# A two-layer hybrid trunk on one core: half-height score passes grouped by head pair, gate rows at full height, and the query norm moved into Exp

## The chip, the cores and the metric

The kernel runs on one core of one Trainium2 chip. The metric is the device time of one execution in microseconds (us). Engines are named as in the profile: PE (TensorE matmul), PEld (its weight loads), DVE (VectorE), ACT (ScalarE), POOL (GpSimd), SP (the queue that issues most DMAs).

## The reference, cut to what matters

Two layers run over 256 latent tokens and 256 context tokens. In each layer three head groups stand side by side: a bidirectional mLSTM (4 heads), a neighbourhood attention with a position bias (NA, 6 heads), and a multi-head latent attention (MLA, 6 heads). Then come an output projection and a feed-forward block (dense in layer 0, top-2-of-8 experts in layer 1). Context outputs of the mixers are needed in layer 0 alone.

```python
# MLA: the queries' norm is one factor for each token
cq = rmsnorm(a[..., :Q_LORA], q_norm_w)          # y = x * rsqrt(mean(x*x) + EPS) * w
qf = (cq @ w_uq).reshape(b_, t_, MLA_H, MLA_NOPE + MLA_ROPE)
...
s_l = einsum(qn_b, kn) + einsum(qr_b, kr)        # latent keys
s_c = einsum(qn_b, knc) + einsum(qr_b, krc)      # context keys
pr = softmax(concatenate([s_l, s_c], -1))
# NA
s = einsum('bhqd,bhrkd->bhqrk', q_r, k_b) + bias
pr = softmax(concatenate([s, einsum('bhqd,bhcd->bhqc', q_r, kc)], -1))
# mLSTM
s = einsum('bhntd,bhnsd->bhnts', qc, kc) * exp(dmat - m_t[..., None])
```

## The kernel before, in words

Work is written in Python in one order, and a scheduler that knows the dependences lays out a fixed order for each engine. Each engine then runs its own list strictly from front to back. So where PE waits for data in a score pass, everything behind it on PE waits too; what keeps PE filled is projection work (the helper `mm3`, lines L93 to L95) which the scheduler puts between score passes and transposes.

Products are made of fp32r halves. For NA and the mLSTM a head has 64 dimensions. Its queries are kept as a tile of 128 rows (`hi`: 64 rows of high halves, 64 rows of low halves, made by `stack_q`), its keys as a tile of 128 rows (the high halves twice) and one of 64 rows (the low halves, made by `stack_k`). A score therefore takes two matmuls into the same PSUM bank: a **full-height pass** over 128 rows and a **half-height pass** over 64 rows. Head 0 of a pair has its half-height pass on rows 0 to 63, head 1 on rows 64 to 127. MLA scores are one fp32 matmul over 128 rows; the profile shows it as two records.

The attention of a pair of heads (`pair_attend`) runs, for each head and each half `tt` of the queries: score passes, softmax (`lat_probs`: maximum on DVE, Exp on ACT, reciprocal and scaling on DVE), four transposes on PE (`transp`, L377), and at the end the product with the values for both heads (`pv`, L364 and L370), in which head 0 writes PSUM rows 0 to 63 and head 1 rows 64 to 127. In layer 0 the context queries follow (`ctx_probs`). Score banks come from `bs`, a ring of two PSUM banks. Names of tiles tell group, layer, pair, head and half: `na0110s` is the score of NA, layer 0, pair 1, head 1, half 0; `na010cs` that of the context queries of head 0; `ma...` is MLA, `ml...` the mLSTM, `...t` a transpose.

The mLSTM needs, for each head and direction, one row of gate values on all 128 partitions: a matmul (`kbb`, L668) of a one-hot column with a 64-row tile `kbt`, 512 columns.

MLA's query norm is a column for each token (`rms_cols`: sums on PE, then eleven small DVE operations in `rstd`, L106 to L118). Before, `lora_rows` turned the column into a row on all partitions (four or two PE matmuls `cq..pr`, L340, and an ACT copy), and two tables `tab` were made of it on DVE (L819, L820). Every query tile is the projection times such a table (L830), so no MLA score can start before the norm is known.

Of the kernel before, what the change touches and what calls it, by code (L numbers as in the profile page):

```python
# [10 lines left out]
F32R = mybir.dt.float32r  # L11
# [3 lines left out]
OP = mybir.AluOpType  # L15
# [3 lines left out]
P = 128  # L19
# [53 lines left out]
def trunk(ctx: ExitStack, tc: tile.TileContext, I, out):  # L73
# [46 lines left out]
    class Stage:  # L120
# [264 lines left out]

        def lat_probs(self, q, k, tt, name, bias):
            s = self.bs(name + "s")
            for i in range(len(q)):
                pe.matmul(s, q[i][:, tt * P:(tt + 1) * P], k[i], start=(i == 0), stop=(i == len(q) - 1))
# [17 lines left out]
        def ctx_probs(self, q, k, name):  # L407
            s = self.bs(name + "s")
            for tt in range(2):
                for i in range(len(q)):  # L410
                    pe.matmul(s[:, tt * NL:(tt + 1) * NL], q[i][:, NL + tt * P:NL + (tt + 1) * P], k[i][:, NL:NT],
                              start=(i == 0), stop=(i == len(q) - 1))
            st = self.stat(name + "st")
            p = self.etile(name + "p")
            dve.tensor_reduce(st[:, 0:2], s.rearrange("p (t k) -> p t k", t=2), AX.X, OP.max, negate=True)
            for tt in range(2):
                c = slice(tt * NL, tt * NL + NL)
                act.activation(p[:, c], s[:, c], AF.Exp, bias=st[:, tt:tt + 1], accum_out=st[:, 4 + tt:5 + tt])
# [6 lines left out]
        def pair_attend(self, q, k, vt, vo, bias, full, name):  # L425
            pts, ptcs = [], []
            for i in range(2):
                pt = self.ptile(f"{name}{i}")
                for tt in range(2):
                    bb = None if bias is None else bias[i][:, (2 - 2 * tt) * 64:(6 - 2 * tt) * 64]  # L430
                    p = self.lat_probs(q[i], k[i], tt, f"{name}{i}{tt}", bb)
                    self.transp(pt, p, 4, tt, f"{name}{i}{tt}")
                pts.append(pt)
                if full:
                    ptc = self.ptctile(f"{name}{i}")
                    p = self.ctx_probs(q[i], k[i], f"{name}{i}c")
                    for tt in range(2):
                        self.transp(ptc, p[:, tt * NL:(tt + 1) * NL], 2, tt, f"{name}{i}c{tt}")
                    ptcs.append(ptc)
            o = self.bo(name + "o")  # L440
            n = self.pv(pts, ptcs, vt, vo, o)
            return o, n
# [45 lines left out]
        def layer(self, l, r, h=None, done=None):  # L488
# [167 lines left out]
            for j in range(2):  # L656
                pts, ptcs = [], []
                for i in range(2):
# [6 lines left out]
                    for d in range(2):  # L665
                        c = 4 * d + hd
                        kbb = self.bs(f"{nm}kb{d}")
                        pe.matmul(kbb, selr[:64, c:c + 1].to_broadcast([64, P]), kbt, start=True, stop=True)  # L668
                        dve.tensor_reduce(st[:, 4, d, 0:1], kbb[:, NL:NT], AX.X, OP.max)
# [8 lines left out]
                        if full:  # L678
# [7 lines left out]
                            ec.append(e)  # L686
                    for tt in range(2):
                        s = self.bs(f"{nm}s{tt}")
                        for u in range(2):
                            pe.matmul(s, q[u][:, tt * P:(tt + 1) * P], k[u], start=(u == 0), stop=(u == 1))  # L690
                        for d in range(2):
                            e = el[2 * d + tt]
                            dve.tensor_tensor_reduce(out=e, in0=s, in1=e, op0=OP.mult, op1=OP.add, scale=0.125, scalar=0.0,
                                                     accum_out=den[:, d, tt:tt + 1])
                    if full:
                        s = self.bs(f"{nm}sc")
                        for tt in range(2):
                            c = slice(tt * NL, tt * NL + NL)
                            for u in range(2):
                                pe.matmul(s[:, c], q[u][:, NL + tt * P:NL + (tt + 1) * P], k[u][:, NL:],  # L700
                                          start=(u == 0), stop=(u == 1))
                        for tt in range(2):
# [110 lines left out]
            ahead = [na_qk(j) for j in range(l)]  # L813
            rq = lora_rows(self.rms_cols(sq_, nq, 1.0 / 512, self.bs, f"cq{l}"), nq, self.bs, f"cq{l}")
            qs_ = 96.0 ** -0.5
            tabs = [self.ptmp(f"tab{l}{i}")[:, :nq] for i in range(2)]
            for i in range(2):
                a, b = slice(64 * i, 64 * i + 64), slice(64 - 64 * i, 128 - 64 * i)
                dve.tensor_scalar(tabs[i][a], rq[a], qs_, None, op0=OP.mult)  # L819
                dve.scalar_tensor_tensor(tabs[i][b], rq[b], qs_, ct[b, T_R:T_R + nq], op0=OP.mult, op1=OP.mult)  # L820
            for j in range(3):
# [3 lines left out]
                for i in range(2):  # L825
# [5 lines left out]
                    qs.append(t)  # L831
                o, n = self.pair_attend([[q] for q in qs], [[k] for k in K[2 * j:2 * j + 2]], vm, 128 * j, None, full, f"ma{l}{j}")
                mix[5 + j] = self.xbuf(f"ma{l}{j}x")[:, :n]
# [813 lines left out]
```

## Time and profile before

| what | value |
|---|---|
| median of 3 runs | 1792.4 us (1791.77 to 1795.92) |
| the profiled execution | 1796.54 us, span 1794.7 us |
| busy in the span | PE 1738.0 us (97%), PEld 1340.7, DVE 1358.0 (76%), ACT 1012.8 (56%) |
| mean granted PE clock | 0.990 |

Matmul ends are modelled, so PE busy includes cost that is not streaming; the start of one matmul to the start of the next is the better measure of what a matmul costs. The mixer of layer 0 runs from about 60 to 350 us, its feed-forward block to about 760 us, the mixer of layer 1 from about 773 to 1000 us, and the experts from there to the end.

### The profile page before, as it was taken

Reading aid. Unit: us, or ns where it says so; the run is one execution under the profiler, and the core shown is the slowest. Engines: PE = TensorE matmul, PEld = TensorE weight load, DVE = VectorE, ACT = ScalarE, POOL = GpSimd, SP = SyncE. Lnnn points to the kernel's source line nnn. Section 1 sums busy time; section 2 is a strip of 40 time slices with the busy share of each in tenths; the row PEclk is TensorE's granted clock in tenths of the full one; section 3 lists DMA queues with packets and bytes.
Section 4 is the critical chain, followed back from the end, with each engine's and each line's share of the span. In section 5 each row is a group of like instructions: output and inputs, shape, how many; then the busy total and the mean of one; then the engine's idle time right before and its main releaser. Section 6 shows DMA issues by size and latency. Waiting matters only on the chain.

```text
span 1794.7 us, 23711 instructions
## 1 busy us (share of the span) xinstructions
PE 1738.0 (97%) x8636; PEld 1340.7 (75%) x8636; DVE 1358.0 (76%) x2217; ACT 1012.8 (56%) x1418; POOL 3.0 (0%) x9
## 2 busy tenths in 40 slices
PE   6999999999999999999999999999999999999997
PEld 4776766778888888777767788768876787678886
DVE  4757756679987333477777699898989889998885
ACT  3545456542222222355656477786778677877774
POOL 0000000000000000000000000000000000000000
PEclk9999999999999999999999899999999999999998
DMA  9644202227787332322312769899999999999991
GB/s 299 230 156 129 83 25 70 72 72 236 224 314 239 94 94 83 125 91 74 95 56 67 283 257 353 349 420 388 343 372 410 390 350 348 416 410 352 341 361 70
DMA packets 82861, 410.08 MB, mean 228 GB/s; under 512 B 8912, under 2 KB 18640, under 8 KB 48944
## 3 DMA queue, kind: packets, MB, share of 16 engines
q1 hardware_dynamic: 82000, 406.62, 62.0%
q8 instruction: 70, 1.15, 0.3%
q0 software_dynamic: 304, 1.31, 0.2%
q10 hardware_dynamic: 432, 0.55, 0.1%
q14 instruction: 55, 0.45, 0.1%
HBM read 407.40 MB, written 1.05 MB: 228 GB/s over the span
## 4 chain that ended last, share of the span: by engine, by line
PE 85%; DVE 7%; ACT 4%; issue 2%; DMA 2%; SPq 0%; ACTq 0%; DVEq 0%; POOLq 0%
PE ah L1411 6%; PE ah L1412 6%; PE ah L1410 6%; PE ay L1470 3%; PE ay L1469 3%; PE ay L1471 3%; PE ah L1085 1%; PE ah L1088 1%; PE axgp L1265 1%; PE ah L1087 1%; PE ay L1088 1%; PE cq L93 1%; PE nk L93 1%; PE cq L95 1%; PE nk L95 1%
## 5 line engine op out<-in xcount | busy, mean ns | idle before, releaser
L262 DVE CUSTOM_DVE_ANT_0 junk<-awr,crow,sp 128x1024 f32<-128x1024 f32 x80 | 102.6, 1283 | 12.3 <-DMA awr<-adr 10.6
L1438 ACT CAST agh<-atr 128x256 fp32r<-128x256 f32 x55 | 20.5, 372 | 74.3 <-PE atr L1432 74.1
L1309 DVE SCALAR_TENSOR_TENSOR x<-asc,modT,x 128x256 f32<-128x256 f32 x64 | 27.3, 477 | 5.9 <-PE asc L1305 5.9
L1428 ACT ACTIVATE as<-ah 128x256 f32<-128x256 f32 x55 | 21.1, 383 | 10.3 <-PE ah L1412 9.7
L282 PE MATMUL ada<-aw,sc 128*32 128x128 f32 x256 | 13.5, 314 | 13.5 <-ACT Asq L299 11.9
L1324 ACT ACTIVATE ayy<-ay,gslot 128x512 fp32r<-128x512 f32 (+1 forms) x16 | 10.8, 674 | 25.7 <-PE ay L1471 17.5
L1336 ACT CAST aev<-ah 128x512 fp32r<-128x512 f32 x33 | 19.5, 592 | 9.8 <-PE ah L1085 8.0
L1075 DVE TENSOR_TENSOR am_13wl<-am_13w,am_13wh 128x2048 fp32r<-128x2048 f32 x8 | 18.3, 2292 | 7.3 <-ACT am_13wh L1074 7.3
L1075 DVE TENSOR_TENSOR am_21wl<-am_21w,am_21wh 128x2048 fp32r<-128x2048 f32 x8 | 18.3, 2292 | 7.2 <-ACT am_21wh L1074 7.2
L1271 ACT ACTIVATE axh<-axgp,modT 128x256 fp32r<-128x256 f32 (+1 forms) x40 | 16.1, 430 | 13.6 <-PE axgp L1265 10.0
L1439 DVE TENSOR_TENSOR agl<-atr,agh 128x256 fp32r<-128x256 f32 x55 | 23.0, 419 | 0.8 <-ACT agh L1438 0.8
L1429 DVE TENSOR_TENSOR as<-as,ah 128x256 f32<-128x256 f32 x55 | 22.8, 414 | 0.0
L1075 DVE TENSOR_TENSOR am_3wl<-am_3w,am_3wh 128x2048 fp32r<-128x2048 f32 x8 | 18.3, 2286 | 5.6 <-ACT am_3wh L1074 5.6
L282 PEld LDWEIGHTS ada<-aw,sc 128*32 128x32 f32 x256 | 7.3, 121 | 19.6 <-ACT Asq L299 11.9
L1075 DVE TENSOR_TENSOR av_28wl<-av_28w,av_28wh 128x2048 fp32r<-128x2048 f32 x8 | 18.3, 2289 | 4.2 <-ACT av_28wh L1074 4.2
L1075 DVE TENSOR_TENSOR am_11wl<-am_11w,am_11wh 128x2048 fp32r<-128x2048 f32 x8 | 18.3, 2288 | 4.0 <-ACT am_11wh L1074 4.0
L1075 DVE TENSOR_TENSOR av_30wl<-av_30w,av_30wh 128x2048 fp32r<-128x2048 f32 x8 | 18.3, 2286 | 3.5 <-ACT av_30wh L1074 3.5
L1432 PE MATMUL atr<-ck,as 128*128 128x128 f32 x110 | 20.9, 272 | 0.0
L1432 PEld LDWEIGHTS atr<-ck,as 128*128 128x128 f32 x110 | 15.3, 140 | 7.3 <-DVE as L1429 0.4
L1074 ACT CAST am_3wh<-am_3w 128x2048 fp32r<-128x2048 f32 x8 | 15.3, 1907 | 9.6 <-PE ah L1412 5.9
L1075 DVE TENSOR_TENSOR am_2wl<-am_2w,am_2wh 128x2048 fp32r<-128x2048 f32 x8 | 18.3, 2287 | 2.7 <-ACT am_2wh L1074 2.7
L1075 DVE TENSOR_TENSOR av_29wl<-av_29w,av_29wh 128x2048 fp32r<-128x2048 f32 x8 | 18.3, 2287 | 2.5 <-ACT av_29wh L1074 2.5
(6437 smaller groups left out, 6424.7 us busy)
## 6 DMA issues: line engine op xcount, KB each, us to landing
awr<-adr SPq DMA_DIRECT2D x56, 512.0 KB, 4.6
aw<-ada SPq DMA_DIRECT2D x24, 512.0 KB, 5.0
aw<-ada SPq DMA_DIRECT2D x32, 256.0 KB, 6.0
am_0w<-m SPq DMA_DIRECT2D x8, 1024.0 KB, 6.1
am_1w<-m SPq DMA_DIRECT2D x8, 1024.0 KB, 6.5
am_2w<-m SPq DMA_DIRECT2D x8, 1024.0 KB, 6.4
am_3w<-m SPq DMA_DIRECT2D x8, 1024.0 KB, 7.9
am_4w<-m SPq DMA_DIRECT2D x8, 1024.0 KB, 8.3
```

Source lines behind the costliest of these rows:

```text
L93: pe.matmul(ps, a[0], b[0], start=first, stop=False)
L95: pe.matmul(ps, a[1], b[0], start=False, stop=last)
L262: ins = dve.tensor_tensor_reduce(out=junk, in0=w, in1=rows[v], op0=OP.mult, op1=OP.add, scale=1.0, scalar=sp[:, l, b:b + 1], accum_out=mod ...
L1075: dve.tensor_tensor(l[:, c], raw[:, c], f32(h[:, c]), op=OP.subtract)
L1088: pe.matmul(p, x, w[1], start=False, stop=last)
L1410: pe.matmul(p, xh, wH, start=(kt == 0), stop=False)
L1411: pe.matmul(p, xh, wL, start=False, stop=False)
L1412: pe.matmul(p, xl, wH, start=False, stop=(kt == KT - 1))
L1432: pe.transpose(tr[:, u * P:(u + 1) * P], s[:, u * P:(u + 1) * P], ident)
L1469: pe.matmul(yq, gh, wH, start=(f == 0), stop=False)
L1470: pe.matmul(yq, gh, wL, start=False, stop=False)
L1471: pe.matmul(yq, gl, wH, start=False, stop=(f == NF - 1))
```

## The change

It has three parts.

1. **Score passes.** `lat_scores` and `ctx_scores` issue the passes of several scores together: first all full-height ones, then all half-height ones, tied in this order. For NA a group is both heads of a pair and one half of the queries; for the mLSTM it is both halves of one head; the context queries of NA form one group for both heads. A group takes both score banks.
2. **Gate rows.** `kbt` gets 128 rows (the rows added are zeros), and `kbb` is a full-height matmul of the same 512 columns.
3. **MLA's query norm.** `lora_rows` falls away for the queries, `tab` is made of constants alone, and the reciprocal rms `rq` of the query tokens is the `scale` of Exp. The negated maximum has to be multiplied by it first, one DVE operation on one or two columns for each softmax.

```diff
+        def lat_scores(self, items, name):
+            ss = [self.bs(f"{name}{i}") for i in range(len(items))]
+            n = len(items[0][0])
+            self.passes([(s, q[u][:, tt * P:(tt + 1) * P], k[u], u == 0, u == n - 1)
+                         for u in range(n) for s, (q, k, tt) in zip(ss, items)])
+            return ss
+        def ctx_scores(self, items, name):
...
+            self.passes([(s[:, tt * NL:(tt + 1) * NL], q[u][:, NL + tt * P:NL + (tt + 1) * P], k[u][:, NL:],
+                          u == 0 and tt == 0, u == n - 1 and tt == 1)
+                         for u in range(n) for tt in range(2) for s, (q, k) in zip(ss, items)])
...
-                dve.tensor_reduce(st[:, 0:1], s, AX.X, OP.max, negate=True)
-                act.activation(p, s, AF.Exp, bias=st[:, 0:1], accum_out=st[:, 4:5])
+                dve.tensor_reduce(st[:, 1:2], s, AX.X, OP.max, negate=True)
+                dve.tensor_tensor(st[:, 0:1], st[:, 1:2], rq, op=OP.mult)
+                act.activation(p, s, AF.Exp, bias=st[:, 0:1], scale=rq, accum_out=st[:, 4:5])
...
+            both = len(q[0]) > 1
+            for hds in ([(0, 1)] if both else [(0,), (1,)]):
+                for tt in range(2):
+                    ss = self.lat_scores([(q[i], k[i], tt) for i in hds], f"{name}{hds[0]}{tt}s")
+                    for i, s in zip(hds, ss):
+                        lat(i, tt, s)
...
-            kbt = self.tp.tile([64, 512], F32R, tag="kbt", bufs=1, name=f"kbt{l}")
-            act.mul(kbt, self.ct[:64, :512], 0.0)
+            kbt = self.tp.tile([P, 512], F32R, tag="kbt", bufs=1, name=f"kbt{l}")
+            act.mul(kbt, self.ct[:, :512], 0.0)
...
-                        pe.matmul(kbb, selr[:64, c:c + 1].to_broadcast([64, P]), kbt, start=True, stop=True)
+                        pe.matmul(kbb, selr[:, c:c + 1].to_broadcast([P, P]), kbt, start=True, stop=True)
...
-            rq = lora_rows(self.rms_cols(sq_, nq, 1.0 / 512, self.bs, f"cq{l}"), nq, self.bs, f"cq{l}")
+            rq = self.rms_cols(sq_, nq, 1.0 / 512, self.bs, f"cq{l}")
...
-                dve.tensor_scalar(tabs[i][a], rq[a], qs_, None, op0=OP.mult)
-                dve.scalar_tensor_tensor(tabs[i][b], rq[b], qs_, ct[b, T_R:T_R + nq], op0=OP.mult, op1=OP.mult)
+                dve.tensor_scalar(tabs[i][a], ct[a, T_R:T_R + nq], 0.0, qs_, op0=OP.mult, op1=OP.add)
+                dve.tensor_scalar(tabs[i][b], ct[b, T_R:T_R + nq], qs_, None, op0=OP.mult)
```

The mLSTM's own two score loops are replaced by `lat_scores` over its two halves and `ctx_scores` of one head.

Two places show how the engines' lists move. The first is PE in NA of layer 0, the context scores of pair 1. Before, `nk01h` (128 rows) and `nk01l` (64 rows) take turns:

```order
L411 MATMUL na010cs<-nk01h_2716,nq01h_2755 128x256
L411 MATMUL na010cs<-nk01l,nq01h_2755 128x256
L411 MATMUL na010cs<-nk01h_2716,nq01h_2755 128x256
L411 MATMUL na010cs<-nk01l,nq01h_2755 128x256
L389 MATMUL na0110s<-nk01h_2720,nq01h_2758 128x512
```

Of the change, the same scores (`_2856` is head 0, `_2857` head 1; the `nq` rows are projection work):

```order
L390 MATMUL na010cs_2856<-nk01h_2727,nq01h_2766 128x256
L93 MATMUL nq_2959<-h004h,nq02wh 128x512
L94 MATMUL nq_2959<-h004h,nq02wh 128x512
L95 MATMUL nq_2959<-h004h,nq02wl 128x512
L390 MATMUL na010cs_2857<-nk01h_2731,nq01h_2769 128x256
L390 MATMUL na010cs_2856<-nk01h_2727,nq01h_2766 128x256
L390 MATMUL na010cs_2857<-nk01h_2731,nq01h_2769 128x256
L390 MATMUL na010cs_2856<-nk01l,nq01h_2766 128x256
L390 MATMUL na010cs_2857<-nk01l,nq01h_2769 128x256
L390 MATMUL na010cs_2856<-nk01l,nq01h_2766 128x256
L390 MATMUL na010cs_2857<-nk01l,nq01h_2769 128x256
```

The four half-height passes of both heads now stand together, head 0 (rows 0 to 63) and head 1 (rows 64 to 127) in turn.

The second place is the start of MLA in layer 1 on DVE. Before (`cq1r` is the norm as a row, `q_7473` and `q_7488` the projections of the first pair's two heads):

```order
L118 SCALAR_TENSOR_TENSOR cq1rc<-cq1rc 128x2
L191 TENSOR_TENSOR nk11wl<-nk11w,nk11wh 128x1024
L819 TENSOR_SCALAR tab_7461<-cq1r 64x256
L820 SCALAR_TENSOR_TENSOR tab_7461<-cq1r,ctB 64x256
L819 TENSOR_SCALAR tab_7462<-cq1r 64x256
L820 SCALAR_TENSOR_TENSOR tab_7462<-cq1r,ctB 64x256
L830 TENSOR_TENSOR q100t<-q_7473,tab_7461 128x256
L830 TENSOR_TENSOR q100t<-q_7488,tab_7462 128x256
```

Of the change, from the first query tile on:

```order
L858 TENSOR_TENSOR q100t<-q_7479,tab_7467 128x256
L574 SCALAR_TENSOR_TENSOR nq10h_7449<-nq_7421,nq10h_7449 64x256
L112 SCALAR_TENSOR_TENSOR cq1rc<-cq1rc 128x2
L113 SCALAR_TENSOR_TENSOR cq1rc<-cq1rc 128x2
L114 TENSOR_TENSOR cq1rc<-cq1rc 128x2
L858 TENSOR_TENSOR q100t<-q_7494,tab_7468 128x256
L115 TENSOR_TENSOR cq1rc<-cq1rc 128x2
L116 TENSOR_SCALAR cq1rc<-cq1rc 128x2
L117 TENSOR_TENSOR cq1rc<-cq1rc 128x2
L415 TENSOR_REDUCE ma1000st<-ma1000s_7510 128x1
L118 SCALAR_TENSOR_TENSOR cq1rc<-cq1rc 128x2
L191 TENSOR_TENSOR nk11wl<-nk11w,nk11wh 128x1024
```

The query tiles no longer stand behind `cq1rc` (the eleven operations of the norm) and the tables, but among them. The new multiplication of the maximum (L416) is the next row, behind the weight split `nk11wl`.

On PE at this place `cq1pr` and twelve projection matmuls of the next pair (`q110`) stood ahead of `ma1000s`; now `ma1000s` and `ma1001s` follow the second head's projection directly, and those matmuls stand behind them. The DMA queue of SP moves four transfers by a few places and nothing else.

## Rows read from the trace of the kernel before

**Rows 1.** The page, section 4: shares of the chain that ended last, by engine.

```profile
PE 85%; DVE 7%; ACT 4%; issue 2%; DMA 2%; SPq 0%; ACTq 0%; DVEq 0%; POOLq 0%
```

**Rows 2.** Windows: stretch, length, busy PE PEld DVE ACT POOL, PE clock, DMA share, GB/s.

```profile
100.00:350.00 250.00, 248.68 (x1284) 172.10 (x1283) 171.83 (x522) 142.59 (x322) 0.00 (x0) 1.00 0.26 83
908.90:913.00 4.10, 4.03 (x9) 2.18 (x10) 1.92 (x5) 0.78 (x2) 0.00 (x0) 0.58 0.22 85
913.00:1000.00 87.00, 86.42 (x525) 62.10 (x524) 61.22 (x167) 54.99 (x139) 0.00 (x0) 1.00 0.26 82
```

**Rows 3.** Timeline of PE, NA of layer 0 (start, duration, ..., [idle before]).

```profile
277.84 0.39 PE L389 MATMUL na0000s<-nk00h,nq00h 128*128 128x512 f32 x1
278.16 0.49 PE L389 MATMUL na0000s<-nk00l,nq00h 64*128 64x512 f32 x1
278.58 0.50 PE L389 MATMUL na0001s<-nk00h,nq00h 128*128 128x512 f32 x1
279.01 0.50 PE L389 MATMUL na0001s<-nk00l,nq00h 64*128 64x512 f32 x1
279.44 0.50 PE L93 MATMUL nk<-h004h,nk01wh 128*128 128x512 f32 x1
279.79 0.40 PE L94 MATMUL nk<-h004h,nk01wh 128*128 128x512 f32 x1
280.02 0.39 PE L95 MATMUL nk<-h004h,nk01wl 128*128 128x512 f32 x1
```

**Rows 4.** Timeline of PE, two gate rows of layer 1 that follow each other.

```profile
812.06 0.28 PE L95 MATMUL mo<-h106h,mo11wl 128*128 128x256 f32 x1
812.27 0.73 PE L668 MATMUL ml10kb<-kbt,selr 64*128 64x512 f32 x2
812.92 0.50 PE L93 MATMUL kv<-h100h,kv10wh 128*128 128x512 f32 x1
813.27 0.39 PE L94 MATMUL kv<-h100h,kv10wh 128*128 128x512 f32 x1
```

**Rows 5.** Timeline of PE, products with the values, mLSTM, layer 0.

```profile
206.36 0.38 PE L364 MATMUL ml01o<-ml02pt,vml 128*64 128x256 f32 x1
206.37 0.38 PE L364 MATMUL ml01o<-ml03pt,vml 128*64 128x256 f32 x1
206.58 0.38 PE L364 MATMUL ml01o<-ml02pt,vml 128*64 128x256 f32 x1
```

**Rows 6.** Line 690, weight loads: count, ns min/median/max, first and last start.

```profile
L690 PEld LDWEIGHTS ml00s<-cv02sl,cv00sh x2: 183/183/183, 109.9 to 114.9; 64*128 64x128 f32 x2
```

**Rows 7.** Timeline, start of MLA in layer 1.

```profile
904.67 0.36 PE L93 MATMUL q<-cq10h,wq11wh 128*128 128x256 f32 x1
905.87 1.23 DVE L191 TENSOR_TENSOR nk11wl<-nk11w,nk11wh 128x1024 fp32r<-128x1024 f32 x1 [0.36 <-ACT nk11wh L190]
908.97 1.64 PE L389 MATMUL ma1000s<-K,q100t 128*128 128x512 f32 x2 [1.88 <-DVE q100t L830]
910.65 0.69 DVE L393 TENSOR_REDUCE ma1000st<-ma1000s 128x1 f32<-128x512 f32 x1 [1.17 <-PE ma1000s L389]
911.38 0.69 ACT L394 ACTIVATE ma1000p<-ma1000s,ma1000st 128x512 f32<-128x512 f32 x1 [4.69 <-DVE ma1000st L393]
912.97 0.15 DVE L403 RECIPROCAL ma1000st<-ma1000st 128x1 f32<-128x1 f32 x1
```

**Rows 8.** The chain in order of time (start, length, what), where Rows 7 end.

```profile
913.29 0.11 PE q L93
913.41 0.86 PE ma1010s L389 x2
```

**Rows 9.** Timeline, start of MLA in layer 0.

```profile
212.55 1.16 PE L340 MATMUL cq0pr<-ck,cq0rc 128*128 128x128 f32 x8
213.46 0.47 PE L93 MATMUL q<-cq01h,wq01wh 128*128 128x512 f32 x1
218.46 1.13 PE L389 MATMUL ma0000s<-K,q000t 128*128 128x512 f32 x2 [0.43 <-DVE q000t L830]
```

More of the change, by code (lines that the diff above doesn't have):

```diff
@@ L384, in ptctile, with passes, lat_probs @@
             return self.tp.tile([P, 2, NL], F32, tag="ptc", bufs=2, name=name + "ptc")
[L386 to L389, printed above, removed]
+        def passes(self, todo):
+            before = None
+            for out, lhs, rhs, first, last in todo:
+                ins = pe.matmul(out, lhs, rhs, start=first, stop=last)
+                if before:
+                    tc.add_manual_dep(ins.ins, before.ins.name, mybir.DependencyInfo(
+                        mybir.DependencyClass.NoSync, mybir.DependencyReason.DATA), reason="in order")
+                before = ins
+        def lat_scores(self, items, name):
[5 more added lines that the diff above has]
+        def ctx_scores(self, items, name):
+            ss = [self.bs(f"{name}{i}") for i in range(len(items))]
+            n = len(items[0][0])
+            self.passes([(s[:, tt * NL:(tt + 1) * NL], q[u][:, NL + tt * P:NL + (tt + 1) * P], k[u][:, NL:],
+                          u == 0 and tt == 0, u == n - 1 and tt == 1)
+                         for u in range(n) for tt in range(2) for s, (q, k) in zip(ss, items)])
+            return ss
+        def lat_probs(self, s, name, bias, rq=None):
             st = self.stat(name + "st")
@@ L405, in lat_probs, with ctx_probs @@
             return p
[L407 to L412, printed above, removed]
+        def ctx_probs(self, s, name, rq=None):
             st = self.stat(name + "st")
@@ L415, in ctx_probs @@
             dve.tensor_reduce(st[:, 0:2], s.rearrange("p (t k) -> p t k", t=2), AX.X, OP.max, negate=True)
+            if rq is not None:
+                dve.tensor_tensor(st[:, 2:4], st[:, 0:2], rq, op=OP.mult)
             for tt in range(2):
                 c = slice(tt * NL, tt * NL + NL)
-                act.activation(p[:, c], s[:, c], AF.Exp, bias=st[:, tt:tt + 1], accum_out=st[:, 4 + tt:5 + tt])
+                if rq is None:
+                    act.activation(p[:, c], s[:, c], AF.Exp, bias=st[:, tt:tt + 1], accum_out=st[:, 4 + tt:5 + tt])
+                else:
+                    act.activation(p[:, c], s[:, c], AF.Exp, bias=st[:, 2 + tt:3 + tt], scale=rq[:, tt:tt + 1],
+                                   accum_out=st[:, 4 + tt:5 + tt])
             dve.reciprocal(st[:, 8:10], st[:, 4:6])
@@ L423, in ctx_probs, with pair_attend, lat, ctx_ @@
             return p
[L425 to L428, printed above, removed]
-                for tt in range(2):
[L430 to L433, printed above, removed]
-                if full:
[L435 to L439, printed above, removed]
+        def pair_attend(self, q, k, vt, vo, bias, full, name, rq=None):
+            pts, ptcs = [self.ptile(f"{name}{i}") for i in range(2)], []
+            def lat(i, tt, s):
+                bb = None if bias is None else bias[i][:, (2 - 2 * tt) * 64:(6 - 2 * tt) * 64]
+                p = self.lat_probs(s, f"{name}{i}{tt}", bb, None if rq is None else rq[:, tt:tt + 1])
+                self.transp(pts[i], p, 4, tt, f"{name}{i}{tt}")
+            def ctx_(i, s):
+                p = self.ctx_probs(s, f"{name}{i}c", None if rq is None else rq[:, 2:4])
+                for tt in range(2):
+                    self.transp(ptcs[i], p[:, tt * NL:(tt + 1) * NL], 2, tt, f"{name}{i}c{tt}")
+            if full:
+                ptcs = [self.ptctile(f"{name}{i}") for i in range(2)]
+            both = len(q[0]) > 1
[4 more added lines that the diff above has]
+                        lat(i, tt, s)
+                if full:
+                    for i, s in zip(hds, self.ctx_scores([(q[i], k[i]) for i in hds], f"{name}{hds[0]}cs")):
+                        ctx_(i, s)
             o = self.bo(name + "o")
@@ L686, in layer @@
                             ec.append(e)
[L687 to L690, printed above, removed]
+                    ss = self.lat_scores([(q, k, tt) for tt in range(2)], f"{nm}s")
+                    for tt, s in enumerate(ss):
                         for d in range(2):
@@ L695, in layer @@
                     if full:
[L696 to L701, printed above, removed]
+                        s, = self.ctx_scores([(q, k)], f"{nm}sc")
                         for tt in range(2):
@@ L831, in layer @@
                     qs.append(t)
-                o, n = self.pair_attend([[q] for q in qs], [[k] for k in K[2 * j:2 * j + 2]], vm, 128 * j, None, full, f"ma{l}{j}")
+                o, n = self.pair_attend([[q] for q in qs], [[k] for k in K[2 * j:2 * j + 2]], vm, 128 * j, None, full, f"ma{l}{j}", rq)
                 mix[5 + j] = self.xbuf(f"ma{l}{j}x")[:, :n]
```

## The prediction, made before the change ran

> **What bounds the kernel now.** I read the chain of waits first. It runs through PE for 85% of the span [rows 1]. Then I read windows over the mixers, where the change lies: in layer 0, from 100 to 350 us, PE is busy 248.68 of 250 us at full clock, DVE 172, ACT 143; at the end of layer 1's mixer 86.42 of 87 us [rows 2]. The DMA engines are a quarter busy there. So what counts is what PE's list costs, and where it stands still. For that I read the timeline from start to start, since a busy PE may be one that streams nothing.
>
> Full-height passes of 512 columns that follow each other start 0.23 us apart (279.79 to 280.02) [rows 3]. Where a half-height pass stands between them the steps are 0.32, 0.42, 0.43, 0.43 and 0.35: from 277.84 to 279.79 five passes take 1.95 us in place of 5 x 0.234 = 1.17. No row of these has idle time in brackets. Two excursions to half height cost 0.78, so one costs 0.39 and one change of shape 0.195. That it is the change and not the half-height pass itself which costs is seen in the gate rows: from 812.06 to 813.27 stand one pass of 256 columns and three of 512, 0.82 us of streaming, and the time is 1.21: again 0.39 more, though two half-height passes lie in this one excursion [rows 4].
>
> **The change, part by part.** I counted shapes over PE's whole list. Stretches of half-height passes fall from 74 to 33: the gate rows lose theirs, NA has one for each group in place of one for each pass, and so has the mLSTM. The products with the values and other narrow ones are split up five times more. All changes of shape together fall from 293 to 227. The 66 fewer, at 0.195 each: **-12.9 us**. The bounds: 0.165, if the step of 0.35 after the return is left out (1.60 - 4 x 0.234 = 0.66 for four changes), and 0.20, the excess of a step of 0.43 [rows 3]: -10.9 to -13.2.
>
> Passes of two heads on opposite halves of the rows have no row in this trace. The nearest are the products with the values, in which two heads use opposite halves of the columns: the second starts 0.01 us behind the first, and the next couple 0.21 later [rows 5]. So I let such half-height passes share their time: in PE's list eight couples of 512 columns stand side by side (four more are parted by transposes), and six of 256. 8 x 0.22 + 6 x 0.11 = **-2.4 us**; the other end is 0. The Trainium skill ("TensorE: Matmul & The Clock Gate", Part 3 on packing small matmuls) gives about 4 ns between starts on different row groups; no run here shows it yet.
>
> The gate rows at full height stream the same 512 columns, so the matmul itself costs what it did. Clearing 128 rows in place of 64 is one ACT operation for each layer, over the same columns: 0.
>
> MLA, layer 1: PE waits 1.88 us before `ma1000s` for the query tile, which on DVE stands behind the norm, a weight split of 1.23 us and the tables [rows 7]. Then the clock is down: 0.58 on average from 908.9 to 913 [rows 2], that is mostly the lower of the two levels (1.2 of 2.4 GHz), right behind the 1.88 us in which PE stood still. From 904.67, where the next pair's projection starts, to `ma1010s` at 913.41 go 8.7 us [rows 7, 8]. Of the change, two scores of 0.86 and 18 passes of 0.12 lie in between [rows 8]: 3.9 us. A new wait takes some back. The bank of `ma1010s` comes free when the Exp of `ma1000s` is done, and that stands behind the maximum (0.69), the split `nk11wl` (1.23) and the new multiplication (0.15, the price of the reciprocal), then takes 0.69 [rows 7]: from 905.7, some 3.2 us with the last of the norm and the gaps, to about 909.1, where PE is ready at 908.6. 0.5 us there, about 0.4 before the first transposes, and 0.1 of latency: 8.7 - 3.9 - 1.0 = **-3.8 us**. Bounds: 0 (the stall comes back at the bank) and -4.8.
>
> MLA, layer 0: the matmuls of `cq0pr` fall away (212.55 to 213.46), and the wait of 0.43 before `ma0000s` [rows 9]: -1.3. But the norm of the mLSTM's second pair now stands on DVE among the first softmaxes, eleven operations of 0.15, so I take **-1.0**; bounds +1 and -1.3.
>
> The new multiplication stands in 30 softmaxes (18 in layer 0, 12 in layer 1) between the maximum and Exp. At 0.15 [rows 7] that is 4.5 us if nothing covers it. What covers it are projection matmuls and the other scores on PE; it is bare where a bank is waited for. Between 0 and +4.5 I take a third: **+1.5**.
>
> Groups take both score banks, so the second full-height pass waits until the bank before last has been read, and PE's list waits with it: projections, transposes, and behind them the ACT copies and the products with the values. There are 27 groups (12 and 3 in NA, 8 and 4 in the mLSTM). The scheduler puts projection work between the two full-height passes, as the order of `na010cs` shows. The nearest price is the 0.43 that a score waits for DVE in [rows 9], and in [rows 3] no score waits at all. One group in eight with 0.43: **+1.5**. Bounds: 0 and 0.43 in half of them, +6.
>
> Sum: -12.9 - 2.4 - 3.8 - 1.0 + 1.5 + 1.5 = -17.1. The profiled execution took 1796.54 us, so its like would take 1779.4. The median of the runs is 4.1 us below the profiled execution; against it I forecast 1792.4 - 17.1 = **1775.3 us**. What is saved reaches the end: the feed-forward block and the experts follow the mixers and are no shorter or longer for starting sooner.
>
> **The rivals.**
>
> *Half-height passes do not share (1780).* If the second head's pass waits for the first, the 2.4 us are gone. If in addition a weight load cannot hide behind a pass on the same rows, each of the mLSTM's 12 groups, which have two half-height passes on the same rows, pays a load of 0.18 [rows 6]: +2.2. For this stands that no couple on row halves has run here. Against it stands that full-height passes start 0.23 apart though each has a load of its own, so loads do hide behind passes on the same rows [rows 3], and that the two gate rows on the same rows cost no more than one excursion [rows 4]. 1775.3 + 4.6 = 1779.9. The Trainium skill has such a rule (the same page and part: loads overlap matmuls in flight only when the row group differs); the rows contradict it as far as they go.
>
> *The price lies in the half-height pass, not in the change of shape (1784).* Then grouping saves nothing and the gate rows alone gain, 14 of the 74 stretches, 12 of them single: 14 x 0.39 = 5.5 in place of 12.9, and no time is shared: -5.5 - 3.8 - 1.0 + 3.0 = -7.3, so 1785. [Rows 4] speak against it, with one place.
>
> *The score banks become the limit (slower).* A bank is held for a maximum and an Exp, 0.69 each, some 1.4 us [rows 7]. Before, one score was computed while the other was read. If the scheduler's cover is misjudged and each of 27 groups waits a whole hold, that is 38 us in place of the 1.5: 1775.3 + 36 = 1812. It ends slower than before if a group waits on average over 17.1 + 1.5 = 18.6 / 27 = 0.7 us, half a hold. For it speaks that PE's order is fixed and that ACT and DVE often have other work first; against it the projection work in between, and that DVE and ACT have a third of the mixers' time free [rows 2].
>
> *The gain is given back later (1788).* The fixed orders downstream were laid out anew too. If a transfer or a weight split there is what ends a wait, most of the 17 us turns into a longer wait: a quarter left, 1788. Against it: DMA engines are a quarter busy in the mixers [rows 2], and DMA is 2% of the chain [rows 1].
>
> **How the numbers follow.** The forecast 0.63, with its own range from 1771 (the best ends: -13.2, -2.4, -4.8, -1.3, and no waits) to 1780; no sharing 0.13; price in the pass 0.08; banks 0.08, half of it at or above the time before; given back 0.08. The range reaches from 1767 (the best ends, less the 4 us by which runs of one kernel lie apart) to 1785: it holds the first three cases, about 0.82. Changes under 0.3% (5.4 us, 1787.0 to 1797.8) can't be told from none. Faster: the first three, and part of the others, 0.87. Same: most of the given back and some of the banks, 0.09. Slower: the rest of the banks, 0.04.
>
> **What the profile will show.** Right: couples of half-height scores of NA that start 0.01 us apart; steps of 0.23 through each group and 0.32 to 0.43 only at its edges; `cq..pr` gone; `ma1000s` of layer 1 without a bracket, and the clock at 1.00 behind it. The mixer of layer 0 would be about 10 us shorter, that of layer 1 about 7. Wrong: brackets before the second full-height pass of a group, with DVE or ACT named; half-height passes of the two heads 0.2 apart; a lower clock somewhere in the mixers, where PE has come to stand still.

## The result, and the profile after

| | median | range, runs | against the kernel before |
|---|---|---|---|
| before | 1793.77 us | 1791.77 to 1795.92, 4 | |
| changed | 1780.57 us | 1777.92 to 1782.26, 4 | 0.9924, 95% interval 0.9912 to 0.9936 |

The kernel is 13.2 us faster (1793.77 - 1780.57), 4 us less than the 17.1 of the sum; 1780.57 lies inside the range given. The profiled execution took 1782.26 us. The page of the profile after, first its busy times, then the chain by engine, which answers to [rows 1]:

```profile
PE 1722.5 (97%) x8624; PEld 1336.2 (75%) x8624; DVE 1359.9 (76%) x2247; ACT 1013.7 (57%) x1416; POOL 3.0 (0%) x9
PE 85%; DVE 6%; ACT 5%; DMA 2%; issue 1%; SPq 0%; ACTq 0%; DVEq 0%; POOLq 0%
```

PE is 15.5 us less busy (1738.0 before), DVE and ACT as busy as before, and PE holds the chain as it did. Windows after, which answer to [rows 2]:

```profile
100.00:350.00 250.00, 248.22 (x1318) 175.54 (x1315) 175.98 (x545) 146.89 (x324) 0.00 (x0) 1.00 0.27 87
...
894.50:897.90 3.40, 3.40 (x14) 2.88 (x13) 2.25 (x11) 1.42 (x2) 0.00 (x0) 0.50 0.28 111
898.00:901.30 3.30, 3.26 (x22) 2.43 (x20) 2.94 (x7) 0.87 (x2) 0.00 (x0) 1.00 0.07 10
901.30:988.00 86.70, 85.20 (x521) 61.68 (x522) 62.32 (x177) 55.75 (x139) 0.00 (x0) 1.00 0.27 86
```

In the same 250 us of layer 0 PE runs 34 records more (1318 for 1284). In layer 1 a stretch at the lower of the clock's two levels (0.50, 1.2 of 2.4 GHz) has moved: it runs from 894.5 to 897.9, ahead of `ma1000s` (896.72, below) and into that score; from 898.0 on the clock is at 1.00.

The timeline of PE after, an NA group of layer 0, which answers to [rows 3]:

```profile
275.31 0.40 PE L95 MATMUL nk<-h004h,nk01wl 128*128 128x512 f32 x1
275.54 0.39 PE L390 MATMUL na0000s<-nk00h,nq00h 128*128 128x512 f32 x1
275.86 0.49 PE L390 MATMUL na0000s<-nk00l,nq00h 64*128 64x512 f32 x2
276.29 0.50 PE L93 MATMUL nk<-h006h,nk01wh 128*128 128x512 f32 x1
276.62 0.39 PE L94 MATMUL nk<-h006h,nk01wh 128*128 128x512 f32 x1
```

The two half-height passes stand in one row (x2); listed one by one they start at 275.86 and 275.87, 0.01 us apart as forecast. From their start to the next pass go 0.43 us, which was the step of one such pass in [rows 3], and from 275.54 to 276.62 four passes take 1.08 us, 0.14 more than 4 x 0.234.

The timeline of PE after, gate rows of layer 1, which answers to [rows 4]:

```profile
804.79 0.28 PE L95 MATMUL mo<-h106h,mo11wl 128*128 128x256 f32 x1
804.90 0.62 PE L702 MATMUL ml10kb<-kbt,selr 128*128 128x512 f32 x2
805.36 0.39 PE L93 MATMUL kv<-h100h,kv10wh 128*128 128x512 f32 x1
805.59 0.39 PE L94 MATMUL kv<-h100h,kv10wh 128*128 128x512 f32 x1
```

From 804.79 to 805.59 are 0.80 us for 0.82 of streaming; in [rows 4] it was 1.21.

The timeline after, start of MLA in layer 1 (PE, DVE and ACT), which answers to [rows 7, 8]:

```profile
891.42 1.23 DVE L191 TENSOR_TENSOR wq12wl<-wq12w,wq12wh 128x1024 fp32r<-128x1024 f32 x1
892.67 0.69 DVE L562 CAST nk10h<-nk 64x512 fp32r<-64x512 f32 x1
893.38 0.69 DVE L563 TENSOR_TENSOR nk10l<-nk,nk10h 64x512 fp32r<-64x512 f32 x1
894.22 0.36 PE L93 MATMUL q<-cq10h,wq10wh 128*128 128x256 f32 x1 [1.97 <-DVE nk10l L563]
896.72 1.60 PE L390 MATMUL ma1000s<-K,q100t 128*128 128x512 f32 x2
899.03 1.22 DVE L191 TENSOR_TENSOR nk11wl<-nk11w,nk11wh 128x1024 fp32r<-128x1024 f32 x1
900.16 0.15 DVE L416 TENSOR_TENSOR ma1000st<-ma1000st,cq1rc 128x1 f32<-128x1 f32 x1
900.35 0.78 ACT L417 ACTIVATE ma1000p<-ma1000s,ma1000st,cq1rc 128x512 f32<-128x512 f32 x1 [2.52 <-DVE ma1000st L416]
901.27 1.12 PE L390 MATMUL ma1010s<-K,q100t 128*128 128x512 f32 x2
```

`ma1000s` has no bracket any more. But an earlier wait is still there: a pass of the first pair's second projection waits 1.97 us for a bank that `stack_k`'s operations of `nk10` read on DVE, behind a weight split of 1.23. It stood in the trace before too, and the prediction passed over it:

```profile
903.18 0.35 PE L93 MATMUL q<-cq10h,wq10wh 128*128 128x256 f32 x1 [1.97 <-DVE nk10l L529]
913.25 0.59 PE L389 MATMUL ma1010s<-K,q100t 128*128 128x512 f32 x1
```

From there to `ma1010s` went 10.07 us; now it is 7.05 (901.27 - 894.22). The waits of PE after, in layer 1's mixer (us in total, times, longest):

```profile
PE q L93 <- DVE nk10l L563: 2.0, 1, 2.0
PE na1101t L377 <- DVE na1111st L425: 0.8, 1, 0.8
PE ml120t L377 <- DVE ml12e L745: 0.7, 1, 0.7
PE ml121t L377 <- ACT ml12pt L378: 0.7, 1, 0.7
PE ml10s L390 <- ACT ml10e L710: 0.5, 1, 0.5
```

Where the time of the mixers went is seen in a sum over all of PE's rows, from the first gate row to the last product with `wo`. For each pass the step to the next start was compared with the step of the same form among its like (0.234 us for 512 columns, 0.175 for 384, 0.117 for 256, 0.43 for an MLA score record, 0.11 for a transpose or a product with the values). What a step has too much goes to "half" if the pass or a neighbour is half-height, to "narrow" if one is a product with the values or another pass of 64 or 32 columns or rows; brackets that name another engine go to "wait", steps at half clock to "clock". The runs below stand in the same table (us):

```
                          layer 0                             layer 1
                length  half narrow wait clock other  length  half narrow wait clock other
before           278.1  20.0  11.2   1.3   0    2.7    199.3  11.5   8.4   6.8  1.9   5.4
changed          268.9   6.9  14.6   1.7   0    3.5    194.7   4.9   9.3   6.8  1.5   7.3
e1 scores only   279.9   9.5  15.6   5.4  2.4   4.0    197.7   8.2   9.2   7.7   0    7.2
e2 gate only     277.4  17.5  11.2   2.3   0    3.3    197.3   9.7   8.3   7.0  1.6   5.5
e3 norm only     279.1  19.6  13.8   1.1   0    2.4    196.1  11.7   8.3   5.5   0    5.7
e4 NA by head    269.3   9.5  12.7   1.5   0    3.4    194.8   5.3   9.4   6.8  1.6   6.8
e5 no norm       278.8   6.9  15.6   5.5  3.3   4.4    196.4   5.5   9.2   7.8  1.6   6.9
e6 no mLSTM gr.  272.9  10.1  16.9   0.9   0    2.8    194.7   6.9   8.6   6.2  2.0   6.0
e7 no mult.      270.6   6.8  15.8   1.7   0    4.0    194.2   5.1   9.0   6.7  1.6   6.9
e8 ACT copies    268.7   6.6  15.3   1.1   0    3.4    190.8   4.9   9.2   5.9   0    5.9
e9 no scores     277.3  17.2  14.0   1.1   0    2.9    196.0  10.0   8.3   5.8  1.6   5.5
e12 no gate      270.6   9.4  14.6   1.4   0    3.1    195.0   7.5   9.3   6.0   0    7.3
```

Second profiles of two of these kernels (e10 of the changed one, e11 of e8) differ from the first by at most 0.4 us in a length. Layer 0's mixer is 9.2 us shorter, layer 1's 4.6; forecast were about 10 and 7. At half-height passes 19.7 us are gone (20.0 + 11.5 - 6.9 - 4.9), and narrow passes give 4.3 back (3.4 and 0.9).

### The profile page after: what moved, and what is told of

It reads as the page before. It is cut to its first block, busy times and chain, and to the rows that moved or that the text cites. A ratio compares the mean times of both kernels' runs of the same rounds, so it can differ in the third digit from the quotient of the medians.

```text
span 1780.4 us, 23702 instructions
## 1 busy us (share of the span) xinstructions
PE 1722.5 (97%) x8624; PEld 1336.2 (75%) x8624; DVE 1359.9 (76%) x2247; ACT 1013.7 (57%) x1416; POOL 3.0 (0%) x9
## 3 DMA queue, kind: packets, MB, share of 16 engines
q0 software_dynamic: 304, 1.31, 0.2%
## 4 chain that ended last, share of the span: by engine, by line
PE 85%; DVE 6%; ACT 5%; DMA 2%; issue 1%; SPq 0%; ACTq 0%; DVEq 0%; POOLq 0%
PE ah L1439 6%; PE ah L1440 6%; PE ah L1438 6%; PE ay L1498 3%; PE ay L1497 3%; PE ay L1499 3%; PE ah L1113 2%; PE ah L1116 1%; PE ah L1115 1%; PE axgp L1293 1%; PE ay L1116 1%; PE nk L94 1%; PE nk L93 1%; DMA aw<-ada 1%; PE ada L229 1%
## 5 line engine op out<-in xcount | busy, mean ns | idle before, releaser
L262 DVE CUSTOM_DVE_ANT_0 junk<-awr,crow,sp 128x1024 f32<-128x1024 f32 x80 | 102.6, 1283 | 13.0 <-DMA awr<-adr 11.6
L1456 ACT ACTIVATE as<-ah 128x256 f32<-128x256 f32 x55 | 21.1, 384 | 10.3 <-PE ah L1440 9.7
L1460 PEld LDWEIGHTS atr<-ck,as 128*128 128x128 f32 x110 | 15.3, 140 | 7.3 <-DVE as L1457 0.3
L1370 ACT ACTIVATE as<-ah 128x256 f32<-128x256 f32 x33 | 12.9, 391 | 12.8 <-PE ah L1368 12.4
```

What stands on the lines that cost most here:

```text
L262: ins = dve.tensor_tensor_reduce(out=junk, in0=w, in1=rows[v], op0=OP.mult, op1=OP.add, scale=1.0, scalar=sp[:, l, b:b + 1], accum_out=mod ...
L1460: pe.transpose(tr[:, u * P:(u + 1) * P], s[:, u * P:(u + 1) * P], ident)
```

## The experiments

The parts are named score groups, gate rows and query norm. Each run's ratio is to runs of the kernel before on the same chip; a difference of ratios is turned into us by 1794.

### One part at a time

**Score groups alone (e1).** Gate rows and query norm are put back:

```diff
-            kbt = self.tp.tile([P, 512], F32R, tag="kbt", bufs=1, name=f"kbt{l}")
+            kbt = self.tp.tile([64, 512], F32R, tag="kbt", bufs=1, name=f"kbt{l}")
...
-            rq = self.rms_cols(sq_, nq, 1.0 / 512, self.bs, f"cq{l}")
+            rq = lora_rows(self.rms_cols(sq_, nq, 1.0 / 512, self.bs, f"cq{l}"), nq, self.bs, f"cq{l}")
```

> Only the grouping of the score passes (NA pairs and mLSTM); gate rows over 64 rows and the query norm as before. In this kernel PE's list has 264 changes of shape (293 before, 227 with the whole change) and 13 couples of opposite halves. Theory 1 (my sum, all terms true): 29 x 0.195 = -5.7, sharing 8 x 0.22 + 5 x 0.11 = -2.3, banks +1.5: -6.5 us against before, 0.9964. Theory A (what was missing of the gain went into waits behind the grouped scores, +4 in place of +1.5): -4, 0.9978. Rival B (it went missing in the query norm): as theory 1.

Measured: 1795.45 us, ratio 1.0005 (0.9995 to 1.0014). Alone, the largest part of the change is worth nothing. All theories were wrong on it, by nearly 5 us and more. The table shows the 13.8 us saved at half-height passes (10.5 and 3.3), and where they went: 5.2 to narrow passes, 5.0 to waits. The largest wait, before `ma0000s` in layer 0, is 3.9 us where it was 0.43 [rows 9], and the clock was half for 6.8 us around its end (2.4 us lost there).

**Gate rows alone (e2).** The scores are issued pass by pass again (NA head by head, `ctx_scores` likewise, the mLSTM by its own loops as before, and nothing ties the order), and the query norm is put back as in e1. Cut to two places:

```diff
-                          u == 0 and tt == 0, u == n - 1 and tt == 1)
-                         for u in range(n) for tt in range(2) for s, (q, k) in zip(ss, items)])
+                          u == 0, u == n - 1)
+                         for tt in range(2) for s, (q, k) in zip(ss, items) for u in range(n)])
...
-            both = len(q[0]) > 1
+            both = False
```

> Only the gate rows over 128 rows; scores and query norm as before. 270 changes of shape in place of 293. Theory 1 and both others: 23 x 0.195 = -4.5 us, 0.9975; no wait is touched. If the price lay in the half-height pass itself and not in the change of shape, the four half-height passes of each of the layers' gate groups would give at most 0.2 each, and the excess at the edges (0.39 for each excursion) would stand where it was beside the passes that remain half high.

Measured: 1790.81 us, ratio 0.9981 (0.9970 to 0.9991), -3.4 us. In the table 4.3 of the half-height excess are gone (2.5 and 1.8), near the 4.5.

**Query norm alone (e3).** Scores as in e2, gate rows as in e1:

```diff
-                        pe.matmul(kbb, selr[:, c:c + 1].to_broadcast([P, P]), kbt, start=True, stop=True)
+                        pe.matmul(kbb, selr[:64, c:c + 1].to_broadcast([64, P]), kbt, start=True, stop=True)
```

> Only the query norm as the scale of Exp; gate rows and scores as before. 303 changes of shape in place of 293 (the narrow passes fall elsewhere): +2.0. Theory 1: -3.8 - 1.0 + 1.5 + 2.0 = -1.3 us. Theory A: the same. Rival B (the first stall of the second pair's projection stays and pulls the clock down, and the multiplications are bare): -3.0 at the start of layer 1's attention, nothing or a loss in layer 0, +3 from multiplications and +2.0 from shapes: +2 us. Both say within 0.3%; the stretch from the first q101 pass to ma1010s (10.07 us before, 7.05 with the whole change) and the waits behind the new multiplication tell them apart.

Measured: 1792.87 us, ratio 0.9992 (0.9982 to 1.0001), -1.4 us, as theory 1 said; B's +2 is outside the interval. Layer 1's mixer is 3.2 us shorter, layer 0's 1.0 longer, with 2.6 more at narrow passes.

The three together would give 0.9 - 3.4 - 1.4 = -3.9 us; the whole change gives -13.2. So the parts depend on each other.

### The whole change without one part

**Without the query norm (e5):**

```diff
-                o, n = self.pair_attend([[q] for q in qs], [[k] for k in K[2 * j:2 * j + 2]], vm, 128 * j, None, full, f"ma{l}{j}", rq)
+                o, n = self.pair_attend([[q] for q in qs], [[k] for k in K[2 * j:2 * j + 2]], vm, 128 * j, None, full, f"ma{l}{j}")
...
-            rq = self.rms_cols(sq_, nq, 1.0 / 512, self.bs, f"cq{l}")
+            rq = lora_rows(self.rms_cols(sq_, nq, 1.0 / 512, self.bs, f"cq{l}"), nq, self.bs, f"cq{l}")
```

> The whole change without its third part: score groups and gate rows as changed, the query norm as before (rows through cq0pr into the tables). 237 changes of shape in place of 227: +2.0 us. Theory C (the parts depend on each other: with grouped scores the norm comes late on DVE and PE stands still at ma0000s, as it did for 3.87 us with the grouping alone, where the clock then fell for 6.8 us): 4 of wait and 2.4 of low clock in layer 0, 3 at the start of layer 1's attention, 2.0 of shapes: +11 us against the whole change, near 1791.5. Rival, the parts add up: the third part alone gave -1.1 against before, so +1 to +2, near 1782.

Measured: 1791.85 us, ratio 0.9994 (0.9985 to 1.0003): nothing of the whole gain is left, as theory C said, and the third part is worth 12.6 us here and 1.4 alone. The mixers of the table are 11.6 us longer than with the whole change; 4.8 of it are waits (3.8 in layer 0) and 3.4 clock. Its timeline of PE and DVE in layer 0, where MLA begins:

```profile
209.62 0.16 DVE L118 SCALAR_TENSOR_TENSOR cq0rc<-cq0rc 128x4 f32<-128x4 f32 x1
...
212.71 0.38 PE L370 MATMUL ml01o<-ml02ptc,vml 128*64 128x256 f32 x1
...
213.52 1.06 PE L340 MATMUL cq0pr<-ck,cq0rc 128*128 128x128 f32 x8
...
216.03 0.41 DVE L846 TENSOR_SCALAR tab<-cq0r 64x512 f32<-64x512 f32 x1
...
218.68 0.67 DVE L857 TENSOR_TENSOR q000t<-q,tab 128x512 f32<-128x512 f32 x1
...
219.41 2.07 PE L390 MATMUL ma0000s<-K,q000t 128*128 128x512 f32 x2 [3.91 <-DVE q000t L857]
```

and its window behind:

```profile
218.00:226.00 8.00, 6.59 (x23) 3.64 (x24) 5.43 (x16) 0.78 (x2) 0.00 (x0) 0.57 0.00 0
```

The norm is ready on DVE at 209.78. But its next step, `cq0pr`, is a matmul, and on PE's list it stands behind the mLSTM's last products with the values, until 213.52. Then come an ACT copy, four table operations among the mLSTM's own norm, and the query tile: PE stands still for 3.91 us, and the clock falls. In the kernel before, `cq0pr` stood in the same place of the chain, but 5 us of work lay between it and `ma0000s`, and the wait was 0.43 [rows 9]. About half of that work was projection for the next pair; in e5 the same passes had run earlier (the last of them, `q<-cq03h,wq01wl`, at 206.95, in the kernel before at 216.64), so nothing was left to fill the wait. With the query norm in Exp the query tile waits for no matmul: after the whole change `ma0000s` starts at 212.67 right behind its neighbours:

```profile
212.67 1.02 PE L390 MATMUL ma0000s<-K,q000t 128*128 128x512 f32 x2
```

**Without the score groups (e9).** The edit of the scores is that of e2.

> The whole change without its first part: scores one by one as before, gate rows and query norm as changed. 280 changes of shape in place of 227, no couples. If a change of shape is the price: 53 x 0.195 = 10.3 and 2.4 of sharing, less the waits that the groups brought (3.5 by the run without the mLSTM's groups): +9 us against the whole change, near 1789.5. If the price lay in the half-height pass itself, grouping saves nothing, and this kernel is as fast as the whole change or faster: 1777 to 1781.

Measured: 1790.38 us, ratio 0.9976 (0.9965 to 0.9988); the whole change, run again beside it (e10), 1779.66 us, 0.9917 (0.9904 to 0.9931), within what was expected:

> The whole change once more, beside the two others of this call: 0.9924 of before again, within 0.0012.

10.7 us lie between them. So the groups are worth 10.7 us where the query norm cannot hold up PE, and the rival that grouping saves nothing has fallen.

**Without the gate rows (e12).** The edit of the gate rows is that of e1 and e3.

> The whole change without its second part: gate rows over 64 rows as before, score groups and query norm as changed. 254 changes of shape in place of 227. Theory C (only the groups and the query norm depend on each other, through the wait at ma0000s; the gate rows stand alone): 3.4, as the gate rows gave alone, to 27 x 0.195 = 5.3 us more than the whole change, 1783 to 1785, with no wait over 1 us at ma0000s. Rival (each part is lost without both others): near 1791.

Measured: 1783.21 us, ratio 0.9945 (0.9930 to 0.9960), 3.8 us more than the whole change, with no wait at `ma0000s`. In the table 5.1 us more stand at half-height passes (2.5 and 2.6), and 1.5 of clock are missing: in this profile it did not fall in layer 1. Gate rows stand alone (3.4 alone); groups and query norm are what depends on each other.

### Do two half-height passes share their time? (e4)

NA groups of both query halves of one head, and context scores head by head, so that a group's half-height passes use the same rows:

```diff
-            both = len(q[0]) > 1
+            both = False
             for hds in ([(0, 1)] if both else [(0,), (1,)]):
-                for tt in range(2):
+                if len(q[0]) > 1:
+                    ss = self.lat_scores([(q[hds[0]], k[hds[0]], tt) for tt in range(2)], f"{name}{hds[0]}s")
+                    for tt, s in enumerate(ss):
+                        lat(hds[0], tt, s)
+                for tt in range(2 if len(q[0]) == 1 else 0):
```

> The whole change, but each NA group takes the two row halves of one head in place of the same rows of two heads: as many changes of shape (226 against 227), but the two half-height passes of a group use the same rows, so none can share time. Theory 1 and A: the 2.4 us of sharing are lost, +2.4 us against the whole change (1783.0 beside 1780.6); the groups' waits are as many. Rival (half-height passes of two heads do not share time): the same time as the whole change. In the trace the second half-height pass of a group should start 0.22 us behind the first, in place of 0.01.

Measured: 1781.2 us, ratio 0.9925 (0.9909 to 0.9941), the same as the whole change. By the time alone the rival would have won. The timeline of PE says otherwise:

```profile
273.52 0.73 PE L390 MATMUL na000s<-nk00h,nq00h 128*128 128x512 f32 x2
274.19 0.73 PE L390 MATMUL na000s<-nk00l,nq00h 64*128 64x512 f32 x2
274.85 0.50 PE L94 MATMUL nk<-h004h,nk01wh 128*128 128x512 f32 x1
```

Listed one by one, the second half-height pass starts at 274.52, 0.33 us behind the first (0.22 was expected, and on opposite halves it is 0.01). The two take 0.66 us to the next start, on opposite halves 0.43 (above). In the table half-height passes cost 3.0 us more (2.6 in layer 0, 0.4 in layer 1), near the 2.4 forecast. But the scheduler's other order split the products with the values less, and narrow passes of layer 0 cost 1.9 less. An unchanged time can hide two changes of opposite sign.

### What the groups cost

**mLSTM scores one by one (e6)**, its context scores likewise, all else changed:

```diff
-                    ss = self.lat_scores([(q, k, tt) for tt in range(2)], f"{nm}s")
-                    for tt, s in enumerate(ss):
+                    for tt in range(2):
+                        s = self.bs(f"{nm}s{tt}")
+                        for u in range(2):
+                            pe.matmul(s, q[u][:, tt * P:(tt + 1) * P], k[u], start=(u == 0), stop=(u == 1))
```

> The whole change without the grouping of the mLSTM's scores; NA groups, gate rows and query norm as changed. 256 changes of shape in place of 227. Price of a change of shape, no cost of groups: 29 x 0.195 = +5.7 us against the whole change, near 1786.3. Theory A (the mLSTM's groups give much of it back in waits: 0.68 + 0.68 before ml120t and ml121t, 0.67 at vm, about 2 to 3 us in all): +3, near 1783.5.

Measured: 1784.07 us, ratio 0.9940 (0.9926 to 0.9953), 2.9 us more than the whole change. The interval doesn't exclude 5.7, but the table has theory A's balance: 5.2 us more at half-height passes and 1.6 more at narrow ones, and 3.4 less in waits and others (1.4 and 2.0). So the groups of the mLSTM save some 7 us and give half of it back.

**Without the new multiplication (e7):**

```diff
-                dve.tensor_reduce(st[:, 1:2], s, AX.X, OP.max, negate=True)
-                dve.tensor_tensor(st[:, 0:1], st[:, 1:2], rq, op=OP.mult)
+                dve.tensor_reduce(st[:, 0:1], s, AX.X, OP.max, negate=True)
```

> The whole change without the new multiplication between maximum and Exp: the bias of Exp is the maximum itself, and the middle of the reciprocal rms (0.137) stands in the tables, so that the scale is near 1. It is left out that the exponent's largest value is exactly 0; the softmax is unchanged but for rounding on these inputs. 30 multiplications of 0.15. All bare: -4.5 us against the whole change. My term: -1.5. All covered: 0.

Measured: 1781.82 us, ratio 0.9941 (0.9928 to 0.9955): no gain, 1 to 3 us on the slow side by medians or ratios. Layer 0's mixer is 1.7 us longer, 1.2 of it at narrow passes of another order. So all bare (-4.5) is excluded, and no trace of the 1.5 is seen; with the other order beside it, this run does not show that every multiplication is covered.

### The wait that stayed (e8, e11)

`stack_k` copies the high part to the opposite half on ACT:

```diff
                         act.copy(hi[a], p[a])
-                        dve.tensor_copy(hi[hs[1 - i]], p[a])
+                        act.copy(hi[hs[1 - i]], p[a])
```

> The whole change, and in stack_k the copy of the high part to the opposite half on ACT in place of DVE (12 copies of 0.68 on DVE become as many on ACT). In layer 1 the first pass of q101 waits 1.97 us for a bank that the last of these DVE operations frees, and the clock is down for 3.4 us behind it. If that chain on DVE is what holds it: two copies fewer (1.4) leave about 0.6 of the wait and the clock stays up (1.5): -3 us against the whole change. If ACT then is late, the wait stays with ACT named: 0, or some loss in NA, where ACT does the copies and Exp.

> The whole change with the copies of stack_k on ACT, for a comparison with the whole change on one chip. If the wait of 1.97 us and the 3.4 us of low clock behind it are what was left, -3 us against the whole change, as in the profiles' mixer of layer 1 (190.8 against 194.7); if that was one profile's chance, 0.

Measured: 1778.77 us, 0.9915 (0.9901 to 0.9929), and 1777.74 us, 0.9909 (0.9894 to 0.9925). Timeline of PE and one window of the first of the two:

```profile
890.69 0.36 PE L93 MATMUL q<-cq10h,wq10wh 128*128 128x256 f32 x1 [0.55 <-DVE nk10l L563]
892.14 1.02 PE L390 MATMUL ma1000s<-K,q100t 128*128 128x512 f32 x2
...
896.20 1.13 PE L390 MATMUL ma1010s<-K,q100t 128*128 128x512 f32 x2
...
953.12 0.65 PE L364 MATMUL na11o<-na110pt,vna 128*64 128x256 f32 x2 [1.31 <-ACT na110pt L378]
```

```profile
890.80:894.20 3.40, 3.40 (x19) 2.44 (x20) 3.27 (x10) 1.43 (x2) 0.00 (x0) 1.00 0.00 0
```

The wait shrank by 1.42, as two copies of 0.69 would give, and the clock stayed at 1.00. A new wait of 1.31 came up in NA, where ACT is late. Layer 1's mixer took 190.8 us in both profiles, against 194.7 and 194.9 in the two of the whole change: 4 us. Of that 1.8 and 1.9 arrive in the medians (1780.57 - 1778.77 and 1779.66 - 1777.74), 1.6 and 1.4 by the ratios. Part of the rest is seen ahead of that mixer: `pb`, a matmul of the gates, waits 1.68 and 1.70 for DVE in these two profiles, 0.54 and 0.55 in the two of the whole change. With nine runs of each, the ratio of medians has an interval of 0.998 to 1.0005 (by drawing samples from the runs): this version beats the kernel before clearly, the changed kernel only probably.

## Why the prediction was right

**Changes of shape and sharing (-12.9 and -2.4): right.** The two together were -15.3; half-height and narrow passes together gave -19.7 + 4.3 = -15.4. The trace has the stretches that were counted (74 before, 33 after) and the 66 fewer changes. That the sum agrees to 0.1 is partly luck: 41 stretches at 0.39 and the sharing make -18.4 at half-height passes, which leaves +3.1 for the narrow ones, so two misses of 1.3 and 1.2 cancel. Sharing is shown by 0.43 against 0.66 for a couple. The forecast steps of 0.23 through each group did not come inside a couple on the same rows: in e4, from 273.86 to 275.18, four steps are 0.33 each, 0.38 more than 4 x 0.234, again the price of one excursion. Of the rule in the Trainium skill ("TensorE: Matmul & The Clock Gate", Part 3 on packing small matmuls), that loads overlap matmuls in flight only when the row group differs, or else into a background weight buffer, the row group alone does not fit: the full-height passes 0.234 apart have the same rows and a load each. Whether the 0.23 that the same-row couple takes more is a load or the streaming itself, no run separates; it is what one streaming pass takes.

**MLA, layer 1 (-3.8): right in kind, too large.** Measured -3.0, from the first waiting pass to `ma1010s`. The term took only the second of two waits into account. The first, 1.97 us on a bank that DVE reads, stayed, and in the changed kernel half clock stood behind it. The new multiplication stands where it was forecast, behind `nk11wl`, and Exp waits 2.52 for it; but `ma1010s` then has no bracket, so the 0.5 forecast there did not come. (The working slips by 0.2 in two places: 905.7 and 3.2 make 908.9, not 909.1, and `ma1010s` starts at 913.25; 913.41 is where the chain passes to it.)

**MLA, layer 0 (-1.0): right as a difference between the two kernels.** The wait of 0.43 and the matmuls of `cq0pr` are gone, 1.3 us. What no reading of the kernel before could show is that the same edit keeps a wait of 3.9 and a clock at half away, which the groups alone would have brought. The sum held because it was made on the whole change; as a price list of its parts it is wrong.

**New multiplication (+1.5): too large; e7 shows no gain without it.** The third that was taken as bare is not seen.

**Score banks (+1.5): the mis-sized term; about +5.5.** It is a remainder, worked out from the table: the mixers changed by -13.8 (268.9 + 194.7 - 278.1 - 199.3). Take away -15.4, the waits that went (-1.9, -0.4), the clock (-0.4) and the work of `cq..pr` and the like (-1.1: without the five columns the lengths are 242.9 and 165.3 before, 242.2 and 164.9 after), and +5.4 is left: about half in named waits and half in "other" steps, among them the last pass ahead of each wait. That is inside the bounds given (0 to 6), and not where it was looked for: the second full-height pass of a group seldom waits. It is the transposes behind a group that wait, 0.7 each at `ml120t` and `ml121t`, 0.8 at `na1101t`. e6 puts 3.4 of it on the mLSTM; that the other 2.0 come from the NA groups is not shown by a run of their own.

**The rivals.** No sharing: its time was nearest to the result (1780), its mechanism is not what happened; the fit is luck. Price in the pass (its sum gives 1785, though it is headed 1784): fallen by e9, 10.7 us, and by the gate rows' step. Banks as the limit: the mechanism is there, at a fifth of a us for each group, below the 0.7 at which it decides. Given back later: not seen, the end is 14.3 us earlier in the spans (1794.7 to 1780.4). All of this is beside a scatter of the stretches that nothing here touches: the feed-forward block between the mixers took 432.7 and 429.9 us in two profiles of the same changed kernel.

## What to carry to other kernels

Price an edit on the order that the whole change makes: a step that PE has to take in the middle of a chain on DVE cost 0.43 us in one order and 3.9 us and a fallen clock in another, so the edit that removes it looked like 1.4 us alone and was worth 12.6 beside the groups. Where an engine's list is fixed, grouping saves at the passes and asks for it back at the first operations that need the group's results: look for the new brackets there, not at the group. And read every bracket in a stretch before you price one of them; the one left over sets the next limit.

## What was not expected of the hardware

Behind a wait the granted clock did not always fall. Behind the same 1.97 us in layer 1 it was at half for 3.4 us in the changed kernel; in the kernel before it stayed at 1.00 there and fell behind the second wait [rows 2], and in e1 (with both waits of the kernel before), e3 and e12, with the same 1.97, it did not fall in this stretch at all. Windows behind that wait, of before and of e3:

```profile
903.20:908.90 5.70, 3.82 (x28) 3.40 (x28) 4.97 (x17) 1.80 (x3) 0.00 (x0) 1.00 0.31 102
```

```profile
904.00:909.70 5.70, 5.44 (x35) 4.31 (x35) 5.43 (x18) 2.29 (x4) 0.00 (x0) 1.00 0.23 77
```

Behind the 3.9 us of e1 and e5 it fell both times, for 6.8 us; with the wait at 0.55 (e8, e11) it stayed up both times. What decides at 2 us is left open.
